# Expert weights in arms of two tiles, a fourth buffer of high parts, and a routing without GpSimd

## The chip, the cores and the metric

The kernel runs on one core of one Trainium2 chip. The metric is the device time of one execution in microseconds (us). The kernel before takes 1871.7 us, the median of three runs (1870.11 to 1872.2 us).

## The reference

The program is a two-layer decoder trunk for 256 tokens, with 16 learned tokens put ahead of them. Each layer has a mixer with three branches and then a feed-forward part; in the first layer that is a dense SwiGLU, in the second a mixture of eight experts, two to a token. All data is float32. The change touches the second layer's feed-forward part and the layer norm just ahead of it:

```python
def swiglu(t, w_gu, w_down):
    gate, up = jnp.split(t @ w_gu, 2, axis=-1)
    return (jax.nn.silu(gate) * up) @ w_down

def moe_swiglu(x, router_w, router_b, w_gu, w_down):      # 256 tokens of 1024
    logits = t @ router_w + router_b
    top_val, top_idx = lax.top_k(logits, 2)
    top_w = jax.nn.softmax(top_val, axis=-1)
    combine = jnp.sum(jax.nn.one_hot(top_idx, 8) * top_w[..., None], axis=1)
    for e in range(8):                                    # w_gu[e] 1024 x 7168, w_down[e] 3584 x 1024
        out = out + combine[:, e:e + 1] * swiglu(t, w_gu[e], w_down[e])
...
h = layer_norm(ALPHA * h + mix, ln_mix_g[layer], ln_mix_b[layer])
h = layer_norm(ALPHA * h + moe_swiglu(h, ...), ln_ffn_g[layer], ln_ffn_b[layer])
```

The kernel cuts a float32 weight tile into a rounded high part and a low part (the rest), and multiplies tokens by both.

## The kernel before

**Steps and units.** The experts' phase has 56 steps: expert e = step // 7, and j = step % 7 is a slice of 512 of the expert's 3584 inner columns. A step consumes six weight tiles of 128 x 2048 float32 (1 MB each), called units: four "up" units (gate and up weights of its own slice) and two "down" units (of the slice two steps back). `manual_schedule` writes out the order by hand: six slots a step, one unit in each.

**What one unit needs.** SyncE's queue (SP) loads the raw tile into one of 11 buffers (`load_unit`, L1228). ScalarE (ACT) copies the rounded high part out of it (`make_high`, L1252, three buffers). VectorE (DVE) subtracts it from the raw tile for the low part (`make_low`, L1262, three buffers), and this also releases the raw buffer to the next load. TensorE (PE) then multiplies (`products`): high parts at L1274, low parts at L1276.

**Full and half experts.** How many tokens an expert has is known only at run time. An expert with more than 64 tokens is "full": two matmuls for each quarter of a high part. One with up to 64 is "half": one matmul, and its first up unit of a step is "direct" (PE multiplies the raw float32 tile itself, L1288; no parts are made). A register branch around each unit selects on PE, ACT and DVE; before the change, each unit has its own branch on PE. With these inputs experts 0, 3, 4 and 7 are full, 1, 2, 5 and 6 half.

**The work between units.** Two up units fill a PSUM bank; ACT copies it out (`evict`, L1311), PE transposes it (`turn`, L1317), ACT and DVE add its halves (`second` L1321, `total` L1325); silu (L1329), `product` (L1332) and the split of the result (`inner`, L1343 and L1345) follow. A step begins, for the table below, at its silu on ACT, which comes once in each step.

**Dispatch and combine.** `dispatch` gathers the tokens of two coming experts: for each of eight blocks of 128 columns, PE multiplies a selection matrix with the tokens' high and low parts (`xth`, `xtl`; L1176) into a PSUM bank, and ACT copies that into `xe` (L1179, L1183). Experts 0 and 1 are dispatched at the start, each further pair during the odd expert ahead of it, by `tick` in slots 1 and 5, two blocks at a time, through the two banks `ps_tp` that the transposes also use. `combine` (L1376) brings an expert's result back to its tokens during j = 1 and 2 of the next expert.

**Ahead of the experts.** The last layer norm (`norm`: L988 to L994, whose bias add is GpSimd's), the router scores, the top-2 selection (`route`, L1101 to L1156) and the first dispatch stand in a serial chain. `split_first` makes the parts of the first unit, the second half of it on GpSimd. After the routing GpSimd also makes one half of `xtl` (L1491) and multiplies the residual by ALPHA (L1495).

Of the kernel before, what the change touches and what calls it, by code (L numbers as in the profile page):

```python
# [36 lines left out]
WA, WB = 12, 8  # L37
RAWS = "ABBABABAABC"
# [63 lines left out]
class Builder:  # L102
# [814 lines left out]
    def mix_out(self, l):  # L917
# [68 lines left out]
        def norm(t):  # L986
            x = self.oa[:, t, :]
            pin(nc.vector.bn_aggr(mv[:, t, :], st[:, t].rearrange("p a b -> p (a b)")))  # L988
            pin(nc.vector.scalar_tensor_tensor(x, x, mv[:, t, 0:1], gb[0], OP.subtract, OP.mult))
            pin(nc.scalar.activation(rs[:, t, :], mv[:, t, 1:2], AF.Ln, bias=self.eps))  # L990
            pin(nc.scalar.activation(rs[:, t, :], rs[:, t, :], AF.Exp, scale=-0.5))
            pin(nc.vector.scalar_tensor_tensor(nm[:, t, :], mv[:, t, 0:1], -1.0, rs[:, t, :], OP.mult, OP.mult))
            pin(nc.scalar.activation(x, x, AF.Copy, scale=rs[:, t, :]))
            pin(nc.gpsimd.tensor_add(x, x, gb[1]))  # L994

        early = []
        for hf in range(2):
# [3 lines left out]
            for t, i in ((0, 0), (1, 0), (0, 1), (0, 2), (1, 1), (0, 3), (1, 2), (1, 3)):  # L1001
# [6 lines left out]
                if hf and t == 1 and i == 2:  # L1008
                    early += self.split_first(2, nc.gpsimd)
                    take(ps, 0, 1)  # L1010
                    norm(0)
# [10 lines left out]
        norm(1)  # L1022
        self.high.append([h for h, _ in early])
        self.low.append([x for _, x in early])
        self.route(pl, rs, nm)

    def split_first(self, kk, eng=None):

        r = self.raws[0].rearrange("p (k n) -> p k n", n=512)
        hv, lv = self.split(r[:, kk : kk + 2, :], 2, 512, self.tc.keep_in_program_order, eng)  # L1030
        return [(hv[:, i, :], lv[:, i, :]) for i in range(2)]
# [53 lines left out]
    def route(self, pl, rs, nm):  # L1085
# [38 lines left out]
        self.warm(WB)  # L1124
        V.scalar_tensor_tensor(self.pos, pr[:, : 2 * E].rearrange("p (a b) -> p a b", a=2), 1.0, mask,
# [32 lines left out]
    def dispatch(self, e0):  # L1158
# [86 lines left out]
    def make_high(self, k):  # L1245
# [4 lines left out]
        with self.if_split(k, mybir.EngineType.Activation):  # L1250
            for v in self.pieces(k):
                self.nc.scalar.activation(hi[:, v], self.raws[k][:, v], AF.Copy)  # L1252
        self.whole[k] = hi
        self.high.append([hi[:, c : c + 512] for c in range(0, 2048, 512)])

# [10 lines left out]
    def products(self, k, full, parts, first, last):  # L1266
# [3 lines left out]

        def some(cases):
            for i, ((ps, x), hv) in enumerate(zip(parts, self.high[k])):
                for c, a in enumerate(cases(x)):
                    mm(ps, a, hv, start=i in first and c == 0, stop=False)  # L1274
            for i, ((ps, x), lv) in enumerate(zip(parts, self.low[k])):
                mm(ps, cases(x)[0], lv, start=False, stop=i in last)  # L1276

        whole = lambda x: (x[:, 0, :], x[:, 1, :])
        both = lambda x: (x.rearrange("p a n -> p (a n)")[:, 0 : 2 * P : 2],)
        if full is None:  # L1280
            some(whole)
        else:
            with self.tc.If(full[mybir.EngineType.PE] > 0) as case:
                some(whole)
            with case.Else():
                if self.direct(k):
                    for i, (ps, x) in enumerate(parts):
                        mm(ps, rr(both(x)[0]), self.raws[k][:, i * 512 : i * 512 + 512], start=i in first, stop=i in last)  # L1288
                else:
                    some(both)  # L1290

    def experts(self, base, first):
# [55 lines left out]
        def unit(k):  # L1348
            kind, i, q = self.units[k]
            e, j = steps[i]  # L1350
            if kind == "up":
                half, q = divmod(q, 2)
                if q == 0:
                    ps[i, half] = self.pmm()
                xe = self.slots[e][0]
                self.products(k, fulls[e], [(ps[i, half], xe[:, 4 * q + x]) for x in range(4)],
                              (0,) if q == 0 else (), (3,) if q else ())
            else:
                if j == 0 and q == 0:
                    py[e] = [self.pacc(), self.pacc()]  # L1360
                self.products(k, fulls[e], [(py[e][x % 2], f2[i][:, 2 * q + x // 2]) for x in range(4)],
                              (0, 1) if j == 0 and q == 0 else (), (2, 3) if j == NJ - 1 and q else ())
# [26 lines left out]
        with self.tc.manual_schedule():  # L1389
# [3 lines left out]
            while len(self.raws) < 11:  # L1393
# [4 lines left out]
            for i, (e, j) in enumerate(steps):  # L1398

                done = e - 1 if j == 1 else None  # L1400
                after = e - 1 if j == 2 else None
                if j == 2:
                    value(e + 1)
                for slot in range(6):
                    if e % 2 and j == 2 and slot == 2 and e + 1 < N_EXPERTS:
                        self.bg.append(self.dispatch(e + 1))
                    if slot in (2, 3) and i < 2:
                        if slot == 2 and i:
                            turn(i - 1, 1)
                        if slot == 2:  # L1410
                            evict(i, 0)
                        if slot == 3 and i:
                            second(i - 1, 1)
                            total(i - 1, 1)
                        continue

                    if slot in (1, 5):
                        self.tick()
# [4 lines left out]
                    unit(k)  # L1423
                    if slot == 5 and done is not None and done >= 0:
                        combine(done, 0)
                    if slot == 1 and after is not None and after >= 0:
                        combine(after, 1)

                    if slot == 0 and i:
# [4 lines left out]
                    if slot == 3:  # L1434
# [3 lines left out]
                    if slot == 4 and done is not None and done >= 0:  # L1438
                        rows(done, 0, 0)
                    if slot == 0 and after is not None and after >= 0:  # L1440
                        rows(after, 1, 0)

                    if slot == 4 and i:
                        product(i - 1)
                    if slot == 5 and i:
                        inner(i - 1, 1)
                    if slot in (0, 2) and after is not None and after >= 0:
                        add(after, slot // 2)
                    if slot == 4 and done is not None and done >= 0:
                        rows(done, 0, 1)  # L1450
                    if slot == 0 and after is not None and after >= 0:
                        rows(after, 1, 1)
# [4 lines left out]
                    if slot == 3:  # L1457
# [210 lines left out]
```

## Time and profile before

| | |
|---|---|
| median of three runs | 1871.7 us |
| the profiled execution's own time | 1873.42 us |
| its span on the core | 1871.7 us |
| PE busy | 1792.5 us (96%) |
| DVE busy | 1484.5 us (79%) |
| ACT busy | 1240.6 us (66%) |
| GpSimd (POOL) busy | 310.0 us (17%) |
| experts' phase, from the first unit's high part on | from 877 us |

The profiled execution spends 1.7 us outside its span, and lies 1.7 us above the median. A step's length is the distance between the silus of two steps in ACT's timeline. Six units are 6.29 MB of weights. Lengths of a few kinds of step:

| step | us |
|---|---|
| full, nothing beside (e4 j4) | 17.55 |
| half, nothing beside (e2 j3) | 14.64 |
| half with dispatch (e1 j3, j4, j5) | 17.14, 16.66, 17.80 |
| full with dispatch (e3 j3, j4, j5) | 20.39, 20.36, 19.95 |
| full with combine (e4 j2) | 20.62 |

### The profile page before, as it was taken

What the parts mean: (1) busy time and instruction counts of PE and PEld (TensorE: products, weight loads), DVE (VectorE), ACT (ScalarE), POOL (GpSimd) and SP (SyncE); (2) the same over time, 40 slices, a digit from 0 to 9 for tenths busy, and PEclk for the clock granted to TensorE, in tenths of its full rate; (3) what the DMA queues carried; (4) which work ended last, traced back from release to release, by engine and by line L of the source; (5) the groups of instructions that cost most, each with busy time, mean ns of one, the idle gap of its engine ahead of it and who ended that gap; (6) DMA issues with size and microseconds to landing.
All of it is one profiled execution on the core that took longest, in us unless ns stands there. A gap on an engine that the chain in (4) does not pass through costs nothing. (4 is left out here: it accounts for less than half of the span.)

```text
span 1871.7 us, 28639 instructions
## 1 busy us (share of the span) xinstructions
PE 1792.5 (96%) x10763; PEld 1547.6 (83%) x10763; DVE 1484.5 (79%) x1672; ACT 1240.6 (66%) x1621; POOL 310.0 (17%) x385
## 2 busy tenths in 40 slices
PE   7999999899999999998999999999999999999996
PEld 7989999899998999996787666677787776667784
DVE  7796665865567967766788889998889898999987
ACT  5565564644455755644677777787777777878774
POOL 6115731600132228432000000000000000000000
PEclk8999999999999999999999999999999999999998
DMA  5444545355464445567489999998798999999990
GB/s 210 148 148 162 179 160 181 113 181 173 140 207 151 166 156 180 182 206 270 183 358 364 382 364 407 406 419 352 282 374 326 370 374 376 386 409 418 370 365 26
DMA packets 74841, 497.15 MB, mean 266 GB/s; under 512 B 9340, under 2 KB 10924, under 8 KB 17324
## 3 DMA queue, kind: packets, MB, share of 16 engines
q1 hardware_dynamic: 69200, 486.64, 68.1%
q10 hardware_dynamic: 5468, 8.15, 1.5%
q8 instruction: 115, 1.88, 0.4%
q14 instruction: 58, 0.48, 0.1%
HBM read 493.65 MB, written 1.10 MB: 264 GB/s over the span
## 5 line engine op out<-in xcount | busy, mean ns | idle before, releaser
L1262 DVE TENSOR_TENSOR wlo<-raw,mhi 128x2048 fp32r<-128x2048 f32 x308 | 697.2, 2280 | 81.0 <-ACT mhi L1252 80.9
L1252 ACT ACTIVATE mhi<-raw 128x2048 fp32r<-128x2048 f32 x308 | 582.3, 1908 | 36.8 <-PE ps_mm L1274 13.0
L173 DVE TENSOR_TENSOR w<-raw,w 128x1024 fp32r<-128x1024 f32 (+2 forms) x261 | 321.4, 1232 | 167.4 <-ACT w L172 166.3
L199 PE MATMUL ps_mm<-HL,w 128*128 128x272 f32 (+2 forms) x1344 | 393.1, 293 | 0.6 <-DVE t L394 0.3
L201 PE MATMUL ps_mm<-HL,w 128*128 128x272 f32 (+2 forms) x1344 | 386.2, 287 | 0.0
L200 PE MATMUL ps_mm<-HL,w 128*128 128x272 f32 (+2 forms) x1344 | 384.5, 286 | 1.1 <-DVE HL L378 1.1
L172 ACT ACTIVATE w<-raw 128x1024 fp32r<-128x1024 f32 (+2 forms) x262 | 267.4, 1021 | 124.7 <-PE ps_mm L201 89.2
L1274 PE MATMUL ps_mm<-mhi,xe 128*128 128x512 f32 x1224 | 330.2, 406 | 0.2
L1274 PEld LDWEIGHTS ps_mm<-mhi,xe 128*128 128x128 f32 x1224 | 227.5, 191 | 55.2 <-issue 11.5
L199 PEld LDWEIGHTS ps_mm<-HL,w 128*128 128x128 f32 x1344 | 253.1, 188 | 3.7 <-issue 1.4
L200 PEld LDWEIGHTS ps_mm<-HL,w 128*128 128x128 f32 x1344 | 253.4, 189 | 1.7 <-DVE HL L378 1.3
L201 PEld LDWEIGHTS ps_mm<-HL,w 128*128 128x128 f32 x1344 | 252.9, 188 | 0.3 <-DVE w L173 0.2
L1276 PE MATMUL ps_mm<-wlo,xe 128*128 128x512 f32 x780 | 216.5, 399 | 15.1 <-DVE wlo L1262 14.8
L1276 PEld LDWEIGHTS ps_mm<-wlo,xe 128*128 128x128 f32 x780 | 147.7, 192 | 55.3 <-DVE wlo L1262 25.6
L1274 PE MATMUL ps_acc<-mhi,f 128*128 128x512 f32 x672 | 179.7, 402 | 0.2 <-DVE f L1345 0.2
L1562 POOL TENSOR_TENSOR raw<-raw,gb 128x768 f32<-128x768 f32 x1 | 1.8, 1801 | 963.8 <-ACT raw L1552 963.8
L1274 PEld LDWEIGHTS ps_acc<-mhi,f 128*128 128x128 f32 x672 | 124.3, 192 | 24.1 <-DVE f L1345 0.5
L1311 ACT ACTIVATE e<-ps_mm 128x512 f32<-128x512 f32 x112 | 67.1, 599 | 109.0 <-PE ps_mm L1276 107.3
L1276 PE MATMUL ps_acc<-wlo,f 128*128 128x512 f32 x448 | 123.2, 396 | 0.4 <-DVE wlo L1262 0.3
L493 POOL TENSOR_SCALAR seg<-b,ctm 128x16 f32<-128x16 f32 (+3 forms) x96 | 101.5, 1075 | 41.4 <-PE ps_acc L535 21.1
L1276 PEld LDWEIGHTS ps_acc<-wlo,f 128*128 128x128 f32 x448 | 85.0, 192 | 21.2 <-DVE wlo L1262 4.0
L1288 PE MATMUL ps_mm<-raw,xe 128*128 128x512 f32 x224 | 101.0, 594 | 0.8 <-DMA raw<-in_down 0.6
(357 smaller groups left out, 2586.6 us busy)
## 6 DMA issues: line engine op xcount, KB each, us to landing
raw<-in_up SPq DMA_DIRECT2D x224, 1024.0 KB, 7.8
raw<-in_down SPq DMA_DIRECT2D x110, 1024.0 KB, 9.0
raw<-in_g SPq DMA_DIRECT2D x24, 1024.0 KB, 4.9
raw<-in_q SPq DMA_DIRECT2D x12, 1024.0 KB, 5.4
raw<-in_x SPq DMA_DIRECT2D x12, 1024.0 KB, 4.8
raw<-in_dg SPq DMA_DIRECT2D x11, 1024.0 KB, 4.9
raw<-in_du SPq DMA_DIRECT2D x11, 1024.0 KB, 4.8
raw<-in_dd SPq DMA_DIRECT2D x16, 704.0 KB, 4.0
```

The lines of the kernel that those rows point to most:

```text
L172: pin(nc.scalar.activation(hv, src, AF.Copy))
L173: pin((eng or nc.vector).tensor_sub(lv, src, rr(hv)))
L199: nc.tensor.matmul(ps, h, a, start=first and k == 0, stop=False)
L200: nc.tensor.matmul(ps, h, b, start=False, stop=False)
L201: nc.tensor.matmul(ps, lo, a, start=False, stop=last and k == kn - 1)
L493: nc.gpsimd.tensor_scalar(seg[:, j, c0 : c0 + T - l0], ab[:, j, l0:T], self.ctm[:, ki, hd : hd + 1], 0.0, OP.subtract, OP.min)
L1252: self.nc.scalar.activation(hi[:, v], self.raws[k][:, v], AF.Copy)
L1262: self.nc.vector.tensor_sub(lo[:, v], self.raws[k][:, v], rr(self.whole[k][:, v]))
L1274: mm(ps, a, hv, start=i in first and c == 0, stop=False)
L1276: mm(ps, cases(x)[0], lv, start=False, stop=i in last)
L1288: mm(ps, rr(both(x)[0]), self.raws[k][:, i * 512 : i * 512 + 512], start=i in first, stop=i in last)
L1311: ACT(g[i, half], ps.pop((i, half)), AF.Copy)
```

## The change

1. Buffers: one more for high parts (four), one fewer for raw tiles (ten).
2. `pair` takes the place of `unit`: two units of one kind share a branch, an "arm", on PE. They are multiplied in slots 0, 2 and 4.
3. In each slot the high part two units on is made ahead of the slot's evictions, silu and half sums, where it came behind them.
4. `dispatch` yields one block at a time: its matmuls go ahead of an arm in slots 0, 2 and 4, through the four banks `ps_mm` of the sums, and its two copies on ACT go right behind that slot's high part. The first dispatch stands ahead of the first arm as a whole.
5. The routing does without GpSimd: `norm` is cut into `moments`, `centre`, `shift` and `bias`; the centring of the second 128 tokens, the low part of the first unit's second half and a bias add are issued behind the mask's matmuls (`between`). `xtl` is made by DVE alone, and ALPHA is applied by ACT in step 1's empty slots.
6. Fewer warm-up matmuls ahead of the selection (8 for 12), more behind it (10 for 8). At the end the last transposes stand ahead of the last up arm.

The diff, cut to its core:

```diff
-WA, WB = 12, 8
-RAWS = "ABBABABAABC"
+WA, WB = 8, 10
+RAWS = "ABBABABAAB"
...
-        self.rawps["C"] = pool("raw3", RAWS.count("C"))
-        self.hip = pool("ehi", 3)
+        self.hip = pool("ehi", 4)
...
+        def between():
+            centre(1)
+            early.extend(self.split_first(2, hv))
+            bias(0)
+
+        self.route(pl, rs, nm, between)
+        bias(1)
...
         self.warm(WB)
+        between()
         V.scalar_tensor_tensor(self.pos, pr[:, : 2 * E].rearrange("p (a b) -> p a b", a=2), 1.0, mask,
...
         for d in range(KD):
-            if d % 2 == 0:
-                yield
-            ps = self.pacc() if e0 == 0 and d % 4 > 1 else self.ptp()
+            yield
+            ps = self.pmm() if e0 else self.pacc() if d % 4 > 1 else self.ptp()
...
+            if e0:
+                yield
...
+        def some(cases, unsplit):
+            for k, parts, first, last in units:
+                if unsplit and self.direct(k):
+                    for i, (ps, x) in enumerate(parts):
+                        mm(ps, rr(both(x)[0]), self.raws[k][:, i * 512 : i * 512 + 512], start=i in first, stop=i in last)
+                    continue
+                for i, ((ps, x), hv) in enumerate(zip(parts, self.high[k])):
+                    for c, a in enumerate(cases(x)):
+                        mm(ps, a, hv, start=i in first and c == 0, stop=False)
+                for i, ((ps, x), lv) in enumerate(zip(parts, self.low[k])):
+                    mm(ps, cases(x)[0], lv, start=False, stop=i in last)
...
                 for slot in range(6):
-                    if slot in (1, 5):
-                        self.tick()
...
+                    busy = slot % 2 == 0 and e % 2 and e + 1 < N_EXPERTS and (j > 2 or j == 2 and slot == 4)
+                    if busy:
+                        next(nxt, None)
+                    if not idle:
+                        self.make_high(k + 2)
+                    if busy:
+                        next(nxt, None)
                     if slot == 0 and i:
                         evict(i - 1, 1)
                         silu(i - 1)
                     if slot == 2:
                         evict(i, 0)
...
-                    self.make_high(k + 2)
-                    if slot == 4 and i:
-                        inner(i - 1, 0)
-                    self.make_low(k + 1)
...
+                    if not idle:
+                        self.make_low(k + 1)
...
+                    if slot % 2 == 0:
+                        pair(k)
...
-            pin((nc.vector if t else nc.gpsimd).tensor_sub(self.xtl[:, t, :], x, rr(self.xth[:, t, :])))
-        self.make_high(1)
-        self.make_low(1)
-        for t in range(2):
-            nc.gpsimd.tensor_scalar_mul(self.oa[:, t, :], self.oa[:, t, :], ALPHA)
+            pin(nc.vector.tensor_sub(self.xtl[:, t, :], x, rr(self.xth[:, t, :])))
+        self.tc.keep_in_program_order(self.make_high(1))
         self.experts(0, first)
```

Three places show how this moves instructions. The first is ACT's order in one half step without dispatch or combine (expert 6), from the copy of the sums on. `mhi` is a high part, `e` the sums, `ps_mm` a bank of sums; the numbers only tell buffers of one name apart. Before:

```order
L1311 ACTIVATE e_2547_19487<-ps_mm_19406 128x512
L1329 ACTIVATE e_2530_19364<-e_2530_19364 128x512
L1252 ACTIVATE mhi_19490<-raw_19251 128x2048
L1283 UNCONDITIONAL_BRANCH
L1252 ACTIVATE mhi_19517<-raw_19281 128x2048
L1283 UNCONDITIONAL_BRANCH
L1311 ACTIVATE e_2555_19549<-ps_mm_19469 128x512
L1252 ACTIVATE mhi_19551<-raw_19309 128x2048
L1283 UNCONDITIONAL_BRANCH
L1321 ACTIVATE e_2547_19487<-ps_tp_19523 128x4x64
L1252 ACTIVATE mhi_19579<-raw_19336 128x2048
```

The same stretch after:

```order
L1277 ACTIVATE mhi_19330<-raw_19078 128x2048
L1338 ACTIVATE e_2548_19332<-ps_mm_19278 128x512
L1356 ACTIVATE e_2532_19208<-e_2532_19208 128x512
L1314 UNCONDITIONAL_BRANCH
L1277 ACTIVATE mhi_19377<-raw_19094 128x2048
L1277 ACTIVATE mhi_19388<-raw_19145 128x2048
L1314 UNCONDITIONAL_BRANCH
L1338 ACTIVATE e_2557_19390<-ps_mm_19339 128x512
L1277 ACTIVATE mhi_19437<-raw_19155 128x2048
L1348 ACTIVATE e_2548_19332<-ps_tp_19383 128x4x64
```

Each copy of the sums (L1311, now L1338) has moved from ahead of a high part to behind it.

The second is PE's order in expert 3, which dispatches for experts 4 and 5. `sel` is the selection, `xth` and `xtl` the tokens' parts; L1274 and L1276 are products of high and low parts, L1288 the direct ones. Before:

```order
L1283 COMPARE_AND_BRANCH
L1274 MATMUL ps_mm_15295<-mhi_15241,xe_12271 128x512 x8
L1276 MATMUL ps_mm_15295<-wlo_15289,xe_12271 128x512 x4
L1283 UNCONDITIONAL_BRANCH
L1288 MATMUL ps_mm_15295<-raw_14976,xe_12271 128x512 x4
L1283 UNCONDITIONAL_BRANCH
L1176 MATMUL ps_tp_15322<-sel_15044,xth 128x256 x2
L1176 MATMUL ps_tp_15322<-sel_15044,xtl 128x256 x2
L1176 MATMUL ps_tp_15329<-sel_15044,xth 128x256 x2
L1176 MATMUL ps_tp_15329<-sel_15044,xtl 128x256 x2
L1283 COMPARE_AND_BRANCH
```

After:

```order
L1199 MATMUL ps_mm_15219<-sel_14874,xth 128x256 x2
L1199 MATMUL ps_mm_15219<-sel_14874,xtl 128x256 x2
L1314 COMPARE_AND_BRANCH
L1307 MATMUL ps_mm_15235<-mhi_15155,xe_12143 128x512 x8
L1309 MATMUL ps_mm_15235<-wlo_15213,xe_12143 128x512 x4
L1307 MATMUL ps_mm_15235<-mhi_15209,xe_12143 128x512 x8
L1309 MATMUL ps_mm_15235<-wlo_15231,xe_12143 128x512 x4
L1314 UNCONDITIONAL_BRANCH
L1303 MATMUL ps_mm_15235<-raw_14861,xe_12143 128x512 x4
L1307 MATMUL ps_mm_15235<-mhi_15209,xe_12143 128x512 x4
L1309 MATMUL ps_mm_15235<-wlo_15231,xe_12143 128x512 x4
L1314 UNCONDITIONAL_BRANCH
```

Two blocks at once between the units of a pair, through `ps_tp`, have become one block ahead of each arm, through `ps_mm`.

The third is DVE's order in the routing. `rt_` names belong to the top-2 selection, `wlo` is the low part of the second unit. Before:

```order
L1106 TENSOR_REDUCE rt_all<-rt_lg_10249 128x2
L1108 TENSOR_TENSOR rt_eq_1284_10256<-rt_lg_10249,rt_all 128x16
L1109 TENSOR_TENSOR rt_eq_1284_10256<-rt_eq_1284_10256,rt_pri_9976 128x16
L1262 TENSOR_TENSOR wlo_10323<-raw_10014,mhi_10321 128x2048
L1110 TENSOR_REDUCE rt_km_1285_10257<-rt_eq_1284_10256 128x2
L1111 TENSOR_TENSOR rt_all<-rt_pri_9976,rt_km_1285_10257 128x16
```

After, from the same reduction's end to the mask (`rt_mask`) and what stands behind it:

```order
L1134 TENSOR_TENSOR rt_all<-rt_pri_9976,rt_km_1288_10257 128x16
L1140 TENSOR_TENSOR rt_mask_10229<-rt_all 128x16
L992 SCALAR_TENSOR_TENSOR oa<-oa,lt_mv_10031,seg_9999 128x1024
L1053 TENSOR_TENSOR w_10192<-raw_10012,w_10192 128x1024
L999 TENSOR_TENSOR oa<-oa,seg_10000 128x1024
L1149 SCALAR_TENSOR_TENSOR rt_all<-ps_tp_10230,rt_mask_10229 128x16
```

The low part of the second unit has left the selection, and three wide operations stand between the mask (L1140) and the positions (L1149).

## Rows read from the trace of the kernel before

**Rows 1.** The page's busy times, shares of the span and instructions.

```profile
PE 1792.5 (96%) x10763; PEld 1547.6 (83%) x10763; DVE 1484.5 (79%) x1672; ACT 1240.6 (66%) x1621; POOL 310.0 (17%) x385
```

**Rows 2.** Windows: stretch, us, busy PE, PEld, DVE, ACT, POOL, clock, DMA, GB/s.

```profile
870.50:898.00 27.50, 17.51 (x107) 16.15 (x107) 22.72 (x44) 12.73 (x18) 16.93 (x6) 0.75 0.38 141
1063.53:1115.13 51.60, 48.26 (x205) 35.70 (x204) 43.20 (x36) 40.20 (x51) 0.00 (x0) 0.97 0.97 374
1115.13:1237.26 122.13, 114.83 (x465) 83.18 (x464) 112.28 (x80) 98.46 (x93) 0.00 (x0) 1.00 0.99 402
1269.30:1352.19 82.89, 79.43 (x365) 64.42 (x366) 69.84 (x58) 61.12 (x65) 0.00 (x0) 0.98 0.82 322
1404.87:1425.48 20.61, 20.13 (x89) 15.94 (x90) 19.90 (x16) 14.58 (x14) 0.00 (x0) 1.00 0.84 321
1425.48:1495.55 70.07, 70.07 (x320) 57.03 (x319) 60.85 (x40) 53.66 (x49) 0.00 (x0) 1.00 0.90 358
1657.77:1701.64 43.87, 41.62 (x169) 30.21 (x168) 40.06 (x28) 35.83 (x34) 0.00 (x0) 1.00 1.00 409
```

**Rows 3.** ACT's timeline at a step's start: start us, us, operation.

```profile
1425.48 0.62 ACT L1329 ACTIVATE e<-e 128x512 f32<-128x512 f32 x1
```

**Rows 4.** Chain of waits in one half step: start us, us, what.

```profile
1608.65 1.20 PE ps_mm L1276 x4
1609.86 3.43 PE ps_mm L1288 x8
...
1615.67 1.92 ACT mhi L1252
...
1617.61 2.29 DVE wlo L1262
1619.90 0.40 DVE e L1325
...
1620.94 2.29 DVE wlo L1262
...
1623.28 1.20 PE ps_mm L1276 x4
```

**Rows 5.** The loads' line L1228, 1115 to 1237 us: from issue to landing.

```profile
DMA to landing us min/median/max: 5.0/9.8/12.7
```

**Rows 6.** DMA view, 1115 to 1237 us: what the engines moved, in 40 slices.

```profile
GB/s 317 193 430 427 430 408 341 352 430 422 422 406 422 424 424 422 357 414 422 422 403 320 403 424 424 414 392 357 422 419 424 411 422 424 414 419 419 427 411 419
```

**Rows 7.** SP's waits, 1657 to 1702 us: total us, times, longest.

```profile
SPq L1228 <- DVE wlo L1262: 23.3, 12, 2.9
```

**Rows 8.** Timeline of DVE and PE in the routing: start us, us, operation.

```profile
871.45 3.37 DVE L989 SCALAR_TENSOR_TENSOR oa<-oa,lt_mv,seg 128x1024 f32<-128x1024 f32 x1
874.81 0.68 DVE L971 TENSOR_TENSOR oa<-oa,ps_mm 128x512 f32<-128x512 f32 x1
...
880.82 2.29 DVE L1262 TENSOR_TENSOR wlo<-raw,mhi 128x2048 fp32r<-128x2048 f32 x1
883.22 2.12 DVE L1111 TENSOR_TENSOR rt_all<-rt_pri,rt_km 128x16 f32<-128x16 f32 x1
885.37 2.27 DVE L1116 SCALAR_TENSOR_TENSOR rt_cur<-rt_all,rt_lg 128x16 f32<-128x16 f32 x1
...
889.42 0.17 DVE L1117 TENSOR_TENSOR rt_mask<-rt_all 128x16 bf16<-128x16 f32 x1
...
891.73 1.22 DVE L1491 TENSOR_TENSOR xtl<-oa,xth 128x1024 fp32r<-128x1024 f32 x1
...
904.87 1.09 PE L1276 MATMUL ps_mm<-wlo,xe 128*128 128x512 f32 x4
```

**Rows 9.** PE's timeline in expert 3's dispatch; in brackets the wait ahead.

```profile
1293.55 0.39 PE L1176 MATMUL ps_tp<-sel,xth 128*128 128x256 f32 x2
...
1294.49 2.00 PE L1274 MATMUL ps_mm<-mhi,xe 128*128 128x512 f32 x8
...
1307.84 0.50 PE L1176 MATMUL ps_tp<-sel,xth 128*128 128x256 f32 x2 [0.75 <-ACT xe L1183]
```

More of the change, by code (lines that the diff above doesn't have):

```diff
@@ L1021, in mix_out, with split_first @@
         scores(1, 1)
-        norm(1)
+        moments(1)
+        centre(0)
+        shift(1)
+        def between():
[4 more added lines that the diff above has]
+        bias(1)
         self.high.append([h for h, _ in early])
         self.low.append([x for _, x in early])
[L1025 to L1031, printed above, removed]
+    def split_first(self, kk, part=None):
+        nc, pin = self.nc, self.tc.keep_in_program_order
+        r = self.raws[0][:, kk * 512 : kk * 512 + 1024]
+        w = part
+        if part is None or part == "high":
+            w = self.wp.tile([P, 2048], F32R, tag="w", name=self.name("w"))
+            pin(nc.scalar.activation(w[:, :1024], r, AF.Copy))
+        if part == "high":
+            return w
+        pin(nc.vector.tensor_sub(w[:, 1024:], r, rr(w[:, :1024])))
+        return [(w[:, c : c + 512], w[:, 1024 + c : 1536 + c]) for c in (0, 512)]
     def route_begin(self, g, b):
@@ L1264, in make_low, with products @@
         self.load_unit()
-    def products(self, k, full, parts, first, last):
+    def products(self, full, units):
         mm = self.nc.tensor.matmul
[L1271 to L1276, printed above, removed]
         whole = lambda x: (x[:, 0, :], x[:, 1, :])
         both = lambda x: (x.rearrange("p a n -> p (a n)")[:, 0 : 2 * P : 2],)
+        def some(cases, unsplit):
[9 more added lines that the diff above has]
+                    mm(ps, cases(x)[0], lv, start=False, stop=i in last)
         if full is None:
-            some(whole)
+            some(whole, False)
         else:
             with self.tc.If(full[mybir.EngineType.PE] > 0) as case:
-                some(whole)
+                some(whole, False)
             with case.Else():
[L1286 to L1290, printed above, removed]
+                some(both, True)
     def experts(self, base, first):
@@ L1398, in experts @@
             for i, (e, j) in enumerate(steps):
-                done = e - 1 if j == 1 else None
-                after = e - 1 if j == 2 else None
+                done = e - 1 if j == 1 and e else None
+                after = e - 1 if j == 2 and e else None
                 if j == 2:
                     value(e + 1)
+                if e % 2 and j == 2 and e + 1 < N_EXPERTS:
+                    nxt = self.dispatch(e + 1)
                 for slot in range(6):
[L1405 to L1415, printed above, removed]
-                    if slot in (1, 5):
-                        self.tick()
+                    idle = slot in (2, 3) and i < 2
                     if slot == 2 and i:
@@ L1422, in experts @@
                         turn(i, 0)
[L1423 to L1427, printed above, removed]
+                    if slot == 2 and j == 2 and e % 2 and e + 1 < N_EXPERTS:
+                        next(nxt)
+                    busy = slot % 2 == 0 and e % 2 and e + 1 < N_EXPERTS and (j > 2 or j == 2 and slot == 4)
[5 more added lines that the diff above has]
+                        next(nxt, None)
                     if slot == 0 and i:
@@ L1460, in experts @@
                         total(i, 0)
+                    if idle:
+                        continue
+                    if slot % 2 == 0:
+                        pair(k)
+                    if slot == 5 and done is not None:
+                        combine(done, 0)
+                    if slot == 1 and after is not None:
+                        combine(after, 1)
                     k += 1
             last = len(steps) - 1
-            unit(k)
             evict(last, 1)
             silu(last)
+            turn(last, 1)
             self.make_high(k + 2)
+            second(last, 1)
             self.make_low(k + 1)
-            turn(last, 1)
-            second(last, 1)
             total(last, 1)
+            pair(k)
             product(last)
             inner(last, 0)
+            self.make_high(k + 3)
             inner(last, 1)
-            for k in range(k + 1, len(self.units)):
-                self.make_high(k + 2)
-                self.make_low(k + 1)
-                unit(k)
+            self.make_low(k + 2)
+            self.make_low(k + 3)
+            pair(k + 2)
         e = N_EXPERTS - 1
```

71 lines of the change are left out of this document (41 added, 30 removed).

## The prediction

> **What bounds the kernel now.** The page's busy times come first: PE is busy for 96% of the span [rows 1]. That is a mean over stages, so I cut the experts' phase at the silus that mark a step's start [rows 3] and asked for the windows by kind of step [rows 2]. Look at the length of a window beside its PE time, then at the DMA share.
>
> - Full steps with nothing beside: 70.07 us for four, PE busy for all of it. PE is the bound, 17.52 a step.
> - Half steps with nothing beside: 43.87 us for three, PE 41.62, DVE 40.06, ACT 35.83, DMA share 1.00. Nothing but the DMA is quite full.
> - The eight steps from 1115.13 us on (the last of expert 1, all of expert 2): 122.13 us, PE 114.83, DVE 112.28, DMA share 0.99.
> - Expert 1's dispatch, three steps: 51.60 us, PE 48.26. Expert 3's combine and dispatch, four full steps: 82.89 us, PE 79.43.
> - The routing, 27.50 us: PE 17.51 us at a mean clock of 0.75; GpSimd 16.93 us.
>
> The chain of waits tells what holds a half step [rows 4]: a product of low parts and a direct unit on PE (1.20 and 3.43 us), two more products up to 1615.14, the copy of the sums, a high part (1.92), a low part (2.29), a half sum (0.40), a second low part (2.29), and 14.63 us after the first row the same row again. A step is a loop through three engines, in which the high part waits behind the copy and the second low part behind the half sum. The timeline of the routing [rows 8] is a serial chain on DVE.
>
> **The change, part by part.** Times are of the profiled execution, whose own 1873.42 us lie 1.7 above the median; savings are taken off the median, 1871.7.
>
> *Routing.* The centring (L989) takes 3.37 us, in a window where GpSimd is busy for 16.93 of 27.50 us [rows 2], while the wide subtraction of `xtl` takes 1.22 [rows 8]. In the selection stand the second unit's low part, 2.29, and two operations of 2.12 and 2.27 us on 16 columns, the like of which is the mask's 0.17. The change takes the first centring from ahead of L971 (3.4), takes the low part out (2.3), and without GpSimd the two small operations should cost 0.2 (4.0); in all 9.8 us: the mask, at 889.42, comes at about 879.6. Against this come a centring, a half unit's subtraction, two bias adds and the other `xtl` on DVE, five wide operations for 1.22 each, 6.1 us, of which I put 2 beside PE's mask sums. The whole first dispatch (eight blocks of 0.47) stands ahead of the first arm, but most of it did so before. So 9.8 less 4.1: the end of the second unit's products, 904.87 + 1.09 = 905.96 us, moves to about 900.3. −5.7. Bounds: −3, if all five stay in the chain and some small rows stay slow; −9, if most lie beside PE.
>
> *Full steps.* PE leaves nothing idle, and the arms hold the same matmuls. Inside an arm the low parts still come one by one, with a buffer to spare. 0. If that cover is thin, an arm waits for its second low part, up to 2.3 us; I see no row for it, since DVE is busy for 60.85 of 70.07.
>
> *Half steps.* With the high part ahead of the copies, the loop loses its half sum and, by the fourth buffer, one low part and the copy ahead of it: 14.63 − 2.29 − 0.53 − 0.40 = 11.4 us. It is no longer the bound. Next is PE, 41.62/3 = 13.87 a step, if the weights come. A step eats 6.29 MB; the slices reach 430 GB/s at best and 402 in the mean [rows 2, 6], that is 14.63 or 15.65 us. So the engines of the DMA already run at what these steps take, and beyond that a faster step can only draw on tiles that lie ready. How many do? A low part releases its raw tile's buffer, and SP waits for that for 23.3 us of a 45 us stretch [rows 7]: the buffers are full. One of eleven is turned over in 11 × 14.63/6 = 26.8 us, of which 9.8 is landing [rows 5] and 4.2 is high and low part; for 12.8 us the tile lies ready. With ten buffers that is 24.4, and the earlier high part takes another 2.4: some 8 us in reserve, which a stretch of half experts can use up once. Expert 1's dispatch and the eight steps behind it have 51.60 − 48.26 = 3.3 and 122.13 − 114.83 = 7.3 us over PE; together 10.6. Of that I take 5, about half, since the reserve can't be spent to the last tile and three of the steps are held by other things. Experts 5 and 6 repeat the pattern: −5 and −5. Bounds for each: 0, if the DMA gives no more; −10.6, PE's floor.
>
> The Trainium skill (DMA: Bandwidth & Descriptors, "Where 436 GB/s comes from") puts the ceiling of the path into on-chip memory at 435 GB/s. By it a half step could not sustain less than 6.29 MB/435 GB/s = 14.46 us, an estimate that speaks for the next rival but one below; the slices of 430 agree. The same section says that from HBM the memory side binds, at about 358 GB/s. By that these steps would take 17.6 us; the trace shows 14.63, so the measurement decides.
>
> *Expert 3, dispatch and combine.* Its four steps take 82.89, PE 79.43, at a mean clock of 0.98, so about 1.6 at the lower level. By count PE needs 4 × 17.52 = 70.1, eight blocks 3.8 (two take from 1293.55 to 1294.49 [rows 9], 0.47 each) and the combine 1.9 (a step with one has nine matmuls more than a clean one, 89 against 320/4 [rows 2], at some 0.2 us, as two of the dispatch take 0.39 [rows 9]): 75.8, and up to 79.4. The stalls are waits like the 0.75 us at 1307.84, where the second block waits for ACT to empty one of two banks. One block at a time through four banks takes most of these. −5. Bounds 0 (the waits move to the sums' banks) and −6.7.
>
> *Combine in a full step.* 20.61 us for 17.52 + 1.9 = 19.4, in experts 4 and 7. The high part now goes ahead of the combine's work on ACT. −1.5 for both; bounds 0 and −2.4.
>
> *Raw buffers.* Ten for eleven costs nothing as long as landing stays under the reserve. *Warm-up, tail:* a product of last transposes ahead of the last arm costs 0.7 and takes a wait of the same size away. 0, by half a microsecond either way.
>
> Sum: −5.7 − 5 − 5 − 5 − 1.5 = −22.2; 1871.7 − 22.2 = **1849.5 us**. All near ends: −3; all far ends: −9 − 21.2 − 6.7 − 2.4 = −39.3, or 1832.
>
> **The rivals.**
>
> *The DMA holds every half step.* Then the ten microseconds of the half experts go, and −12.2 is left: 1859.5. For it: DMA shares of 0.97 to 1.00 in all their windows, and slices that never pass 430. Against it: tiles lie ready, by the turnover above, and SP waits for buffers.
>
> *The half experts fall to PE's floor.* −21.2 in place of −10, and expert 3 its full −6.7: 1871.7 − 5.7 − 21.2 − 6.7 − 1.5 = 1836.6. For it: reserve of 8 us for a stretch that lacks 10.6. Against it: DVE at 40.06/3 = 13.35 leaves half a microsecond a step to wait in.
>
> *Banks.* Dispatch blocks now share four banks with the up arms: three blocks and two arms a step take five in turn, and each block's bank is given back only behind a high part on ACT. If each of the 24 blocks delays an arm by the 0.75 us of the row, that is +18, and nothing but a little is left: 1867.5. Against it: today's waits are of two banks.
>
> *Starved of raw tiles: slower.* The reserve shrinks from 12.8 to 8 us. When the loads bunch up (SP releases two at a time, after an arm), landing can grow. From about 9.8 + 8 = 18 us of landing on PE waits for weights, and each further microsecond costs 6/10 of one in a step (ten buffers, six a step). At 21 us that is 1.8 us in each of 28 half steps, +50; with the −12.2 that stay that is 1909; at 19 us +17 and 1876. Against it: the longest landing is 12.7.
>
> **How the numbers follow.** Forecast 0.50; DMA holds 0.22; PE's floor 0.12; banks 0.09; starved 0.07. The range goes from 1834, which leaves out the lower part of PE's floor, to 1868, the banks' case: about 0.85 of the chance by these cases, and a little less as some term will be off. A change of 0.2% is 3.7 us, about what a measurement of this kernel can tell from none. The forecast, the DMA's and PE's cases are all faster by more than that (0.84), the banks' half (0.04): 0.88, taken as 0.86 since all of it hangs on one reading. Same: the banks' other half and a weak starvation, 0.07. Slower: 0.07.
>
> **What would show it.** The silus of clean half steps at 14.1 to 14.6 us in place of 14.63, with landing of 10 to 14 us and slices still at most 430 GB/s. If they come at 13.9, PE's floor was right; if at 14.63 with a longer wait for loads, the DMA. The four steps of expert 3 at about 78 us, with no wait of a dispatch matmul for ACT. The mask at about 879.6 and the second unit's end at about 900.3. Full steps at 17.52 still. The prediction is wrong if full steps grow, if a product waits for a raw tile in each half step, or if the routing's operations stay slow without GpSimd.

## The result, and the profile after

The changed kernel takes 1838.09 us (1835.55 to 1840.64), the kernel before 1871.76 beside it: a ratio of 0.9822, interval [0.9805, 0.9839]. That is 33.7 us less where 22.2 were forecast. The profiled execution spends 1837.1 us in its span, 34.6 less than before.

The page's busy times after, which answer to [rows 1]:

```profile
PE 1780.4 (97%) x10759; PEld 1547.5 (84%) x10759; DVE 1481.0 (81%) x1676; ACT 1238.0 (67%) x1623; POOL 292.8 (16%) x379
```

PE makes only four matmuls fewer and is yet busy for 12 us less. The windows by kind of step, in the columns of [rows 2]: the routing; expert 1's dispatch; the eight steps up to the end of expert 2; expert 3's combine and dispatch; a combine in a full step; four full steps; three half steps with nothing beside.

```profile
870.50:898.00 27.50, 21.64 (x122) 19.34 (x121) 21.22 (x61) 15.28 (x23) 0.00 (x0) 0.75 0.26 91
1059.50:1106.40 46.90, 44.78 (x197) 33.73 (x196) 41.71 (x36) 38.57 (x46) 0.00 (x0) 1.00 0.97 392
1106.40:1218.60 112.20, 111.03 (x459) 82.75 (x458) 110.17 (x80) 96.84 (x93) 0.00 (x0) 1.00 1.00 412
1249.80:1329.60 79.80, 76.96 (x366) 63.23 (x366) 69.04 (x58) 60.40 (x66) 0.00 (x0) 1.00 0.94 375
1382.30:1402.10 19.80, 19.41 (x89) 15.67 (x88) 19.73 (x16) 14.40 (x14) 0.00 (x0) 1.00 0.86 343
1402.10:1472.20 70.10, 70.10 (x320) 57.04 (x319) 62.10 (x41) 53.91 (x48) 0.00 (x0) 1.00 0.88 351
1164.60:1204.70 40.10, 40.10 (x168) 30.19 (x167) 39.56 (x28) 35.15 (x34) 0.00 (x0) 1.00 1.01 419
```

Cut at the silus, the 34.6 us come from: up to step 1, 5.4; the rest of expert 0, 0.5; from expert 1 to the second step of expert 3, 13.6; the four steps of expert 3, 3.1, and 0.7 in what follows it up to expert 5; from there to the second step of expert 7, 13.0; then nothing until the last silu, and 1.7 us are lost behind it, 31.5 against 33.2. That loss lies behind the last vector operation, where the results are stored, and it isn't shown to be the change's: of the traces below with the same code there, four have 31.2 to 31.3 us behind the last silu and six 33.0 to 33.3. The stretches of half experts bring 26.6 of 34.6. Of that, 9.9 and 9.8 us lie in the eight steps up to the end of experts 2 and 6; the dispatch steps of experts 1 and 5 give 4.6 and 4.2 more, and their j = 2 takes 1.4 back each time.

The chain of waits in one half step after (start us, us, what):

```profile
1176.64 3.43 PE ps_mm L1303 x8
1180.07 0.94 PE ps_mm L1307 x4
1181.02 0.93 PE ps_mm L1309 x4
1181.95 0.44 PE ps_tp L1344 x4
1182.38 0.93 PE ps_acc L1307 x4
...
1190.27 3.43 PE ps_mm L1303 x8
```

Where [rows 4] went PE, ACT, DVE, DVE, PE, every link is now PE: direct unit to direct unit in 13.63 us instead of 14.63. (The silus of these steps stand only 13.36 apart, as each comes a little earlier in PE's step than the one before; the direct units are the better mark.) The loads (L1253, 1106 to 1219 us) show the price of it:

```profile
DMA to landing us min/median/max: 7.8/13.0/19.2
```

Landing was 5.0/9.8/12.7 before [rows 5]. DMA share is 1.01 and the rate 419 GB/s in the clean half steps: 6.29 MB take 15.0 us at that, so steps of 13.6 outrun their loads. Within the stretch the landing grows; the first row is the dispatch ahead of it (1059 to 1106 us), the second its end (1190 to 1219 us):

```profile
DMA to landing us min/median/max: 4.7/9.0/11.3
DMA to landing us min/median/max: 12.5/16.6/19.2
```

The tiles that lay ready when the stretch began are being used up.

The routing on DVE and PE after, answering to [rows 8]; the last row is the second unit's low products:

```profile
873.15 1.23 DVE L992 SCALAR_TENSOR_TENSOR oa<-oa,lt_mv,seg 128x1024 f32<-128x1024 f32 x1
...
876.22 0.18 DVE L1139 SCALAR_TENSOR_TENSOR rt_cur<-rt_all,rt_lg 128x16 f32<-128x16 f32 x1
...
877.26 0.17 DVE L1134 TENSOR_TENSOR rt_all<-rt_pri,rt_km 128x16 f32<-128x16 f32 x1
877.47 0.17 DVE L1140 TENSOR_TENSOR rt_mask<-rt_all 128x16 bf16<-128x16 f32 x1
...
899.64 1.09 PE L1309 MATMUL ps_mm<-wlo,xe 128*128 128x512 f32 x4
```

The mask stands at 877.47 (forecast 879.6) and the second unit ends at 900.73 (forecast 900.3).

### The profile page after: what moved, and what is told of

It is laid out like the page before. It is cut to its first block, busy times and chain, and to the rows that moved or that the text cites. A ratio compares the mean times of both kernels' runs of the same rounds, so it can differ in the third digit from the quotient of the medians.

```text
span 1837.1 us, 28288 instructions
## 1 busy us (share of the span) xinstructions
PE 1780.4 (97%) x10759; PEld 1547.5 (84%) x10759; DVE 1481.0 (81%) x1676; ACT 1238.0 (67%) x1623; POOL 292.8 (16%) x379
## 4 chain that ended last, share of the span: by engine, by line
PE 87%; DVE 8%; issue 1%; POOL 1%; ACT 1%; DMA 1%; SPq 0%; DVEq 0%; ACTq 0%; POOLq 0%
PE ps_mm L1307 15%; PE ps_mm L198 12%; PE ps_mm L200 12%; PE ps_mm L199 12%; PE ps_mm L1309 9%; PE ps_acc L1307 8%; PE ps_mm L1303 5%; PE ps_acc L1309 5%; DVE wlo L1288 3%; PE ps_tp L1344 2%; DMA raw<-in_q 1%; PE ps_acc L534 1%; PE ps_acc L607 1%; DVE w L172 1%; PE ps_tp L1407 1%
## 5 line engine op out<-in xcount | busy, mean ns | idle before, releaser
L1288 DVE TENSOR_TENSOR wlo<-raw,mhi 128x2048 fp32r<-128x2048 f32 x308 | 692.2, 2279 | 17.1 <-ACT mhi L1277 5.7
L492 POOL TENSOR_SCALAR seg<-b,ctm 128x16 f32<-128x16 f32 (+3 forms) x96 | 101.1, 1071 | 41.8 <-PE ps_acc L534 21.2
L1338 ACT ACTIVATE e<-ps_mm 128x512 f32<-128x512 f32 x112 | 67.0, 598 | 50.0 <-PE ps_mm L1309 49.9
```

Source lines behind the costliest of these rows:

```text
L492: nc.gpsimd.tensor_scalar(seg[:, j, c0 : c0 + T - l0], ab[:, j, l0:T], self.ctm[:, ki, hd : hd + 1], 0.0, OP.subtract, OP.min)
L1288: self.nc.vector.tensor_sub(lo[:, v], self.raws[k][:, v], rr(self.whole[k][:, v]))
L1338: ACT(g[i, half], ps.pop((i, half)), AF.Copy)
```

## The experiments

Each is an edit of the changed kernel unless it says otherwise. As the routing differs by up to 5 us from execution to execution (below), single terms are read from the trace, from the first silu to the last: 894.1 us in the changed kernel, 925.0 before. Each kernel has one trace; the changed kernel's second one has 894.7.

**One branch for each unit.**

```diff
-            self.products(fulls[e], units)
+            for one in units:
+                self.products(fulls[e], [one])
```

> The changed kernel with a branch around each unit again in place of one around an arm of two; all else as changed. Theory (the place of the high part on ScalarE makes the half steps short): clean half steps stay at 13.4 us, the time at 1838 to 1841. Rival (one branch fewer in an arm makes them short): clean half steps go back to 14.0 to 14.6 us, which over some 20 half steps is +13 to +24: 1851 to 1862.

1834.47 us (ratio 0.9794 [0.9778, 0.981]); first to last silu 894.3, direct units follow in the same steps. The branch shared by two units gives nothing here. Two units still stand together in a slot in this run; the run on the kernel before, below, has them apart and keeps direct units 13.6 us apart all the same, so arms are not what shortens the half steps.

**High part behind the copies again.** The four lines with `make_high(k + 2)` and the dispatch's second `next` move from ahead of `evict` to ahead of `product`.

> The changed kernel with the high part issued behind the slot's copies, silu and half sums, as before the change; four buffers and arms stay. Theory (the place of the high part): clean half steps back to 14.0 to 14.6 us, time 1850 to 1862. Rival (the fourth buffer alone does it): 13.4 us and 1838 to 1841.

1854.63 us (0.99 [0.9884, 0.9917]), first to last silu 914.3: 20.3 of the 30.9 us are gone. Clean half steps take 14.63 again, and the chain is that of [rows 4], with the copy of the sums ahead of the high part and the half sum between two low parts:

```profile
1643.76 0.45 ACT e L1338
...
1644.25 1.92 ACT mhi L1277
...
1646.19 2.29 DVE wlo L1288
1648.49 0.40 DVE e L1352
...
1649.52 2.29 DVE wlo L1288
...
1651.86 1.20 PE ps_mm L1309 x4
1653.07 3.43 PE ps_mm L1303 x8
...
1667.69 3.43 PE ps_mm L1303 x8
```

Expert 3's dispatch steps keep 18.85, 18.84 and 19.77 us (20.39, 20.36, 19.95 before), expert 1's 15.12, 15.12 and 17.57 (17.14, 16.66, 17.80). That gain belongs to the dispatch, not to the high part's place. In part it is a shift: of the eight blocks, j = 3 and 4 had four each before and have three each now, the other two standing in j = 2.

**Three buffers of high parts.** `pool("ehi", 4)` becomes `pool("ehi", 3)`.

> The changed kernel with three buffers of high parts in place of four, ten raw tiles still. Theory (place and buffer are both needed: with three, the high part that now stands ahead of the copies waits for the arm's first unit and holds the copies up): clean half steps 14 to 15 us and full steps above 17.55, time 1850 to 1870. Rival (the place alone does it): 13.4 us, 1838 to 1841.

1841.93 us (0.9836 [0.982, 0.9853]), first to last silu 899.2. The clean half steps stay all PE at 13.61 us: here the place alone does it, and the theory misses. What three buffers cost, 5.1 us, lies at j = 2 of experts 3, 4 and 7 (23.97, 20.89 and 21.36 us, against 23.31, 19.85 and 20.24), 2.8 us, and in small pieces elsewhere.

**Only the buffers and the high part's place, put into the kernel before.**

```diff
-RAWS = "ABBABABAABC"
+RAWS = "ABBABABAAB"
...
-        self.rawps["C"] = pool("raw3", RAWS.count("C"))
-        self.hip = pool("ehi", 3)
+        self.hip = pool("ehi", 4)
...
+                    self.make_high(k + 2)
                     if slot == 0 and i:
                         evict(i - 1, 1)
...
-                    self.make_high(k + 2)
                     if slot == 4 and i:
                         inner(i - 1, 0)
```

> The kernel before with only its buffers changed (four of high parts, ten raw tiles) and the high part issued ahead of the copies, silu and half sums; no arms, old dispatch, old routing. Theory (this part alone makes the half steps short): clean half steps 13.3 to 13.6 us, 18 to 25 us off the kernel before: 1848 to 1855. Rival (it needs the pairs too): clean half steps 14 us or more, 1862 to 1872.

1853.64 us (0.9901 [0.9886, 0.9916]): 19 us off the kernel before, with direct units 13.6 us apart. The undoing cost 20.3 us with four buffers in both kernels, the doing alone, with the buffers, gives 19: the high part's place is well over half of the result. In the old dispatch the same edit also costs: j = 3 of experts 1 and 3 takes 18.14 and 22.05 us, 17.14 and 20.39 before. Only the new dispatch brings 15.24 and 18.84.

**Nine raw tiles, and eight.** `RAWS = "ABBABABAA"` and `RAWS = "ABABABAA"`.

> The changed kernel with nine raw tiles in place of ten. Theory (half steps run faster than their loads and live on tiles that lie ready, which just suffice in the changed kernel): the reserve is smaller by one tile, 2.2 us, PE waits for loads at the end of each of the two stretches of half experts, +4 to +7 us: 1842 to 1845. Rival (loads keep up, the reserve is not touched): 1838.

> The changed kernel with eight raw tiles in place of ten. Theory (half steps of 13.6 us outrun loads of 420 GB/s and live on tiles that lie ready; nine were just enough): two tiles fewer are 4.5 us less in reserve than with ten, so in experts 2 and 6 direct units that follow one another at 13.6 us with ten tiles slow to about 15.0 us, the rate of the loads, and the time rises by 4 to 10 us: 1842 to 1848. Rival (loads keep up at any depth): 13.6 us to the end and 1836 to 1839.

With nine 1837.76 us (0.9817 [0.9801, 0.9833]): no difference in the time. First to last silu is 896.9, 2.8 more, all of it from the end of expert 2 to j = 2 of expert 3, where a load stands in the chain; direct units keep their 13.6 us to the end. So nine just hold, and the theory's 4 us are not there. With eight 1841.81 us (0.9843 [0.9827, 0.9859]), first to last silu 901.3, 7.2 more, and the last three half steps of both stretches take 14.62 to 14.98 us from silu to silu, against 13.35 to 13.85 in the changed kernel (whose second trace has 14.95 in one of them). Between direct units only the last distance of each stretch grows, to 14.4. The first row is the DMA's rate there (1190 to 1235 us, columns of [rows 2]); then PE's timeline, where low parts come late; then, from the loads' line (1106 to 1235 us), how long and how often high parts waited for a load, with eight tiles and in the changed kernel; then the chain behind these steps, in which a high part follows a load.

```profile
1190.00:1235.00 45.00, 43.41 (x190) 33.59 (x189) 42.70 (x30) 40.13 (x37) 0.00 (x0) 1.00 1.01 419
```

```profile
1200.96 1.21 PE L1309 MATMUL ps_mm<-wlo,xe 128*128 128x512 f32 x4 [0.52 <-DVE wlo L1288]
...
1215.91 0.51 PE L1309 MATMUL ps_mm<-wlo,xe 128*128 128x512 f32 x1 [1.07 <-DVE wlo L1288]
```

```profile
  ACT mhi L1277: 6.1, 13
  ACT mhi L1277: 0.9, 3
```

```profile
1225.68 15.76 DMA raw<-in_up
...
1241.53 0.04 ACT mhi L1277
```

6.29 MB at 419 GB/s are 15.0 us, about the length of those steps. The half experts do live on a reserve; ten tiles cover it, eight don't.

**Dispatch through the two banks again.** `ps = self.pmm() if e0 else ...` becomes `self.ptp() if e0 else ...`.

> The changed kernel with its later dispatches through the two banks ps_tp again, still one block ahead of each arm. Theory (the four banks take the waits of the dispatch away): expert 3's dispatch steps go from 18.84 us to 19.4 or more, expert 1's and 5's grow by half a microsecond or more, +4 to +8 in all: 1841 to 1846. Rival (one block at a time does it, the banks don't matter): 18.84 us and 1835 to 1839.

1837.18 us (0.9818 [0.9803, 0.9833]), expert 3's steps at 18.84 as in the changed kernel, first to last silu 894.8. The four banks do nothing for the dispatch. Nor does the shared branch, the fourth buffer or the high part's place: 18.84 or 18.85 stands in all those runs. What is left is one block at a time ahead of an arm, three blocks in a step for four; no run put two blocks together again, so that is argued and not shown. My theory of two late banks falls, and with it the rival in which the banks cost time.

**The kernel before without GpSimd in the routing.**

```diff
-            pin(nc.gpsimd.tensor_add(x, x, gb[1]))
+            pin(nc.vector.tensor_add(x, x, gb[1]))
...
-                    early += self.split_first(2, nc.gpsimd)
+                    early += self.split_first(2)
...
-            pin((nc.vector if t else nc.gpsimd).tensor_sub(self.xtl[:, t, :], x, rr(self.xth[:, t, :])))
+            pin(nc.vector.tensor_sub(self.xtl[:, t, :], x, rr(self.xth[:, t, :])))
...
...
-            nc.gpsimd.tensor_scalar_mul(self.oa[:, t, :], self.oa[:, t, :], ALPHA)
...
+                            ACT(self.oa[:, slot - 2, :], self.oa[:, slot - 2, :], AF.Copy, scale=ALPHA)
```

> The kernel before with the routing's work on GpSimd (bias adds, the second half of the first unit's low part, half of xtl) put on VectorE, and ALPHA on ScalarE in step 1, with the order of the routing as before. Theory (GpSimd slows VectorE's operations beside it): the selection's two operations of 2.1 and 2.3 us fall to 0.2, the mask comes 3 us or more earlier although VectorE has more to do, time 1866 to 1870. Rival (it is the order that counts): these operations stay at 2 us, the mask comes no earlier, 1871 to 1876.

1868.89 us (0.9983 [0.9974, 0.9993]). DVE's timeline, against [rows 8]:

```profile
873.54 1.28 DVE L989 SCALAR_TENSOR_TENSOR oa<-oa,lt_mv,seg 128x1024 f32<-128x1024 f32 x1
...
886.29 0.17 DVE L1111 TENSOR_TENSOR rt_all<-rt_pri,rt_km 128x16 f32<-128x16 f32 x1
886.50 0.17 DVE L1116 SCALAR_TENSOR_TENSOR rt_cur<-rt_all,rt_lg 128x16 f32<-128x16 f32 x1
...
887.74 0.17 DVE L1117 TENSOR_TENSOR rt_mask<-rt_all 128x16 bf16<-128x16 f32 x1
```

The same instructions take 1.28 for 3.37, 0.17 for 2.12 and 0.17 for 2.27 us with GpSimd idle. The mask comes only 1.7 us earlier, not 3, since DVE has three wide operations of 1.22 us more ahead of it; the other 10.3 us of the changed kernel's mask come with its new order.

In its trace, 3.0 us shorter than the one before (1868.7 for 1871.7 us), the smaller part is routing: the first silu comes 1.1 us earlier. From silu to silu it has 923.1 us for 925.0, and 1.5 of that difference is j = 2 of expert 3, 20.67 us for 22.19, though the code is the same there. The same eight products, first before, then in this run:

```profile
1270.13 3.55 PE L1274 MATMUL ps_mm<-mhi,xe 128*128 128x512 f32 x8
```

```profile
1268.11 2.12 PE L1274 MATMUL ps_mm<-mhi,xe 128*128 128x512 f32 x8
```

The granted clock is 0.64 from 1269.3 to 1273.3 us in the trace before, so part of that at the lower of its two levels (1.2 for 2.4 GHz, 0.50 for 1.00), and 1.00 in this run. So 1.5 us of what expert 3 takes in the trace before are the clock's and not the code's.

**Combine through the sums' banks.** The one stall over 1 us left at j = 2 of expert 3 in the changed kernel is a transpose that waits for two banks to be added out; its row, from PE's timeline:

```profile
1258.97 0.66 PE L1344 MATMUL ps_tp<-ident,e 128*128 128x128 f32 x4 [1.63 <-DVE oa L1413]
```

```diff
-                sums[e, hf, t] = self.ptp()
+                sums[e, hf, t] = self.pmm()
```

> The changed kernel with combine's sums through the four banks ps_mm in place of the two ps_tp. Theory (in j = 2 the transposes wait 1.6 us for the sums to be added out of their two banks): that wait goes in seven experts, -4 to -11: 1825 to 1833 where the changed kernel stands at 1834 to 1838. Rival (the wait moves to the arms, which need the same four banks): no change.

1830.94 us (0.9783 [0.977, 0.9796]), first to last silu 888.5. The transpose follows at once:

```profile
1252.71 1.09 PE L1407 MATMUL ps_mm<-sel,st 128*128 128x512 f32 x4
1253.64 0.60 PE L1344 MATMUL ps_tp<-ident,e 128*128 128x128 f32 x4
```

The gain lies almost whole in the j = 2 of three experts and not of seven: 20.04 us for 23.31 in expert 3, 19.26 for 19.85 in expert 4, 18.83 for 20.24 in expert 7.

**With more warm-up; with a later dispatch; and the changed kernel once more.** The first two stand on the combine's edit: `WB = 22` for 10; and `if slot == 4 and j == 2` for `slot == 2`, with blocks from `j > 2` on.

> The changed kernel with combine's sums through ps_mm and 22 warm-up matmuls in place of 10 behind the mask's sums. Theory (PE stands idle for 3.55 us ahead of the first dispatch, and the clock is then at its lower level, 0.50 from 885 to 895 us in the changed kernel's trace): the idle time shrinks under a microsecond, the granted clock stays at 1.00, the first step's silu comes 2 to 4 us earlier: 1826 to 1829. Rival (more matmuls hold the dispatch up, or the clock falls all the same): 1830 to 1834.

> The changed kernel with combine's sums through ps_mm and the dispatch begun two slots later: its selection in slot 4 of j = 2, its blocks from j = 3 on. Theory (the loads now bound the stretches of half experts, by the 420 GB/s at which steps of 14.95 us run once nothing lies ready): j = 2 of experts 1 and 5 falls from 19.1 to about 17.5 us, but steps at the end of experts 2 and 6 grow by as much; expert 3's j = 2 keeps its gain of about half a microsecond; total change within 2 us: 1829 to 1832. Rival (PE bounds these stretches): 2 to 4 us are gained, 1826 to 1829.

> The changed kernel itself once more, beside the two above and the kernel before on one chip. Theory (the difference of 3.6 us to the run with a branch around each unit is only the clock in the routing, which differs from run to run): 1834 to 1839, steps from the first silu on as in the first profile. Rival (one branch for two units costs something): 1837 to 1840 every time.

With more warm-up 1830.59 us (1830.28 to 1832.22; 0.9779 [0.9765, 0.9792]), the fastest here, though not told apart from the 1830.94 without it. PE's clock holds, as the windows show (the column ahead of the last two), first of the changed kernel, then of this one; the run with the combine's edit alone has 0.50 and 0.74 there:

```profile
885.00:890.00 5.00, 4.11 (x19) 3.78 (x18) 4.65 (x6) 3.41 (x6) 0.00 (x0) 0.50 0.14 20
890.00:895.00 5.00, 4.53 (x18) 3.97 (x18) 2.82 (x10) 3.36 (x7) 0.00 (x0) 0.50 0.46 190
```

```profile
885.00:890.00 5.00, 2.79 (x19) 2.20 (x19) 5.00 (x6) 3.42 (x6) 0.00 (x0) 1.00 0.01 2
890.00:895.00 5.00, 4.53 (x29) 3.92 (x28) 3.46 (x12) 4.18 (x7) 0.00 (x0) 1.00 0.61 210
```

The 2 to 4 us expected are not there: the first silu comes at 907.4 us, against 907.7 with the combine's edit alone. The dispatch now waits up to 1.80 us for DVE's copies. The later dispatch takes 1832.88 us (0.9788 [0.9775, 0.9802]) and gains nothing; j = 2 of expert 1 is 18.65 us and not 17.5, so what holds that step is not the dispatch, and neither theory's reason is shown. The changed kernel once more is 1836.61 us (0.9808 [0.9795, 0.9822]) with 894.7 from silu to silu; its first silu came at 911.7 us, that of the run with a branch for each unit at 907.4. The difference between those two lies ahead of the experts and, by 1.8 us, behind the last silu; between the silus the shared branch costs nothing either. Yet all runs with a branch for each unit (1833.74 to 1834.68 us) lie below all of the changed kernel's (1835.24 to 1841.08), and one trace of them can't tell whether that is chance.

## Why the prediction was right, and where it was off

The direction and the range held, and so did the mechanism of the largest term; its size did not. The gain was 33.7 us where 22.2 were forecast, near the rival "PE's floor" (1836.6), to which I gave 0.12, and by the sign named ahead (clean half steps at 13.9 us and not at 14.1 to 14.6; they came at 13.4 by the silus, 13.6 by the direct units) that rival was the better account. That its number came so close is partly luck: the half experts gave 26.6 us for its 21.2, expert 3 gave 3.1 for its 6.7.

- **Routing**, −5.7: measured −5.4 at the first silu, and that is luck. The mask came 2.1 us earlier than worked out, the second unit's end 0.4 later: behind the mask PE's clock was at its lower level from 885 to 895 us, and how long it stays there differs between executions, which the sum did not reckon with. Nine more traces have this routing; in eight the clock comes back sooner and the first silu stands at 906.4 to 907.9 us, 7.3 to 8.8 ahead of the trace before; in one it stands at 911.7.
- **Half experts**, −5 for each pair: −13.6 and −13.0. This is the term that was mis-sized, in two places. "Some 8 us in reserve" was worked out with the landing of the stretch itself, 9.8 us, where the reserve is already being used up (8.1 in the dispatch steps just ahead, 1063 to 1115 us), and then cut to five "since the reserve can't be spent to the last tile". It was spent: landing up to 19.2 us with the chain of the clean half steps still all PE, and a reserve of two tiles less was the first to slow the half steps. And PE's floor, called the far bound, was too high: 41.62/3 = 13.87 a step is busy time, in which four low products take 1.20 us behind a wait [rows 4] and 0.93 in the chain after; back to back the step takes 13.60. So the half pairs went past a bound of −10.6 that was none: the eight steps alone gave 9.9, where that bound had 7.3.
- The *mechanism* of that term held: the high part behind the copy was the loop, shown by taking it back (+20.3 us) and by doing it with the buffers alone (−19). The fourth buffer, on which I put part of the loop's loss, wasn't needed in clean half steps.
- **Expert 3**, −5: −3.1, of which 1.5 is the clock in the trace before. Its dispatch steps lost 4.2 us, not by the banks, which the sum named; j = 2 grew by 1.1, and by 2.6 against the 20.67 us of the run without GpSimd in the routing. In that lie two dispatch blocks moved there, some 0.5 us each, and the 1.63 us stall above (0.39 before), which I had not seen. In the trace before, the dispatch's waits for ACT that the term was built on add up to 1.5 us in these four steps.
- **Combine** in full steps, −1.5: −0.8 in expert 4, nothing in expert 7. The stall there is the transposes' two banks, which the change left as they were: with combine's sums in the other four, expert 4's step loses 0.6 us more and expert 7's 1.4.
- **Full steps**, 0: 17.5 us still.
- **Tail**, 0: +1.7 in one execution, one of two values that the same code shows.
- The *DMA holds* rival fell only thanks to the reserve, and the *starved* rival gave the point roughly: 18 us of landing was worked out, and landings of up to 19.2 and 19.5 us in the two stretches came without a wait of PE for weights in the clean half steps.
- Two figures of the working don't come out, and neither changes a reading: 3.4, 2.3 and 4.0 us make 9.7 and not 9.8, and expert 3's far end by its own count, 82.89 − 75.8, is 7.1 and not 6.7.

## What to carry to other kernels

A helper copy that feeds a later stage belongs ahead of an engine's evictions when that stage is the loop that sets the step: follow the chain once round, and look for what stands in it without being needed by it. Buffers ahead of a saturated transfer are a stock: compare how long a stretch outruns its loads with what lies ready when the stretch begins, not in its middle. And a busy time is not a floor; take that from back-to-back rows.

## What the runs showed of the hardware that was not expected

With all engines of the DMA busy, 1 MB loads go on at 419 GB/s over 45 us, though slices reached 430. Small VectorE operations of 0.17 us took 2.1 to 2.3 us in the stretch in which GpSimd was busy, so the delay doesn't scale with their own size. Two of GpSimd's operations in the trace before:

```profile
880.95 4.36 POOL L994 TENSOR_TENSOR oa<-oa,seg 128x1024 f32<-128x1024 f32 x1 [2.40 <-ACT oa L993]
885.27 2.34 POOL L1491 TENSOR_TENSOR xtl<-oa,xth 128x1024 fp32r<-128x1024 f32 x1
```

They end at 885.31 and 887.61 us, the two slow operations of [rows 8] at 885.34 and 887.64. Not every small operation beside GpSimd was held up; the reduction at 883.02 us took 0.17.

And PE's clock fell to its lower level behind 3.55 us of idle time of PE in the changed kernel's routing (0.50 is 1.2 GHz, 1.00 is 2.4), while the run with more warm-up, in which the idle time was 0.87 us, kept it:

```profile
883.87 1.19 PE L1199 MATMUL ps_tp<-sel,xth 128*128 128x256 f32 x4 [3.55 <-DVE at L1216]
```

```profile
884.79 0.48 PE L1199 MATMUL ps_tp<-sel,xth 128*128 128x256 f32 x2 [0.87 <-DVE at L1216]
```

In all ten traces with the changed routing and the shorter warm-up PE has this idle time, 3.55 to 3.60 us, and the granted clock from 885 to 890 us is 0.50 to 0.84.
